# A streaming encoder layer: the high and low halves of the weights kept in memory after the first super-block

## The chip, the cores and the metric

The kernel runs on one core of a Trainium2 chip. The time is that of the device, in microseconds (us), from one execution of the whole program; the number given for a kernel is the median of several executions. The core has five engines that work side by side: PE (matrix products, with its weight loads shown apart as PEld), DVE (vector operations), ACT (activation functions and copies), POOL (general elementwise operations) and SP, which in this kernel does nothing but issue transfers between the large memory and the on-chip buffers. Each engine takes its instructions in the order in which they were written for it, and waits for semaphores that other engines or transfers raise.

## The reference, cut to what matters

One layer of a hybrid encoder on x of 2048 rows by 1024 channels, all in 32-bit floating point:

```python
shift, scale, gate = split(silu(c) @ w_ada + b_ada, 3)
h = rmsnorm(x, pre_g) * (1 + scale) + shift
q_lat, kv_lat, k_rope, gm_in, rw_in, z, g_logit = split(h @ w_in)     # 1024 -> 7712
y_mla = latent attention, 8 heads, chunk-causal                       # w_uq, w_ukv
y_gm  = gated spatial mixing inside blocks of 128 rows
y_rw  = RWKV-7 time mixing, 8 heads of 64, a scan over the rows       # w2, a2
branches = stack([y_mla, y_gm, y_rw]) * silu(z)
proj  = branches @ w_br                                               # 3 x (512 -> 1024)
merged = sum(proj * sigmoid(g_logit))
x = x + gate * rmsnorm(merged @ w_out, post_g)                        # 1024 -> 1024
```

The weights w_in, w_br, w_out, w_uq and w_ukv do not depend on the rows, so every block of rows multiplies by the same ones.

## The kernel before, in words

**Tiling.** The 2048 rows are handled in four super-blocks of 512 rows (`NSB`, `SB`). Activations stand transposed: channels on the 128 partitions, the 512 rows of a super-block along the free axis. A product with a large weight is done by `gemm` (lines 577 to 593): for a block of 128 output columns it takes 512 input channels at a time, one weight tile of 128 partitions x 4 x 128, and issues twelve matmuls on it.

**Twelve, because each factor is split in two.** PE multiplies in a format with fewer bits than 32-bit floats (fp32r). A value is therefore written as a high half, which is the value rounded to that format, and a low half, which is the rest; `mm3` (lines 572 to 575) adds high x high, high x low and low x high. The activations' halves are made once per super-block. The weights' halves are made by `wgran` (lines 562 to 570) every time a tile is used: a transfer of 256 KB from `w_in`, `w_br` or `w_out` into a raw tile `wr`, a copy on ACT into `wh`, and a subtraction on POOL or DVE into `wl` (`split`, lines 554 to 560). There are three buffers of each of `wr`, `wh` and `wl` (`WRB`, `WHB`). A super-block uses 162 such tiles: 120 of `w_in` and two for the rotary key (`rope_key`, lines 784 to 806), 24 of `w_br`, 16 of `w_out`; four super-blocks make 648. The small weights of the attention's projections, in `query`, `keys` and `values` (lines 808 to 854), are loaded, split by `parts` and used in the same way, 14 per super-block.

**Stages.** After a start-up part, each super-block s has a scan stage, `wkv(s)`, and then an attention stage, `attention(s)`; after the last one comes `finish`. In the scan stage a chain of small dependent steps runs for each of four pairs of heads: `prepare`, then `inverses` (on DVE, tiles X and tx, with a round trip through memory before and after it: md, mb, xd, xtb), then `advance` and `states` (matmuls into `pss`, with DVE and ACT between them: QG, UV, S, Y). Beside the chain PE does gemms of the projections, of the gates and of the branches' outputs. In the attention stage scores, softmax and weighted sums are on the chain, and gemms of the next super-block's inputs fill in.

**Order.** PE's instructions are in an order written out when the program is built: the class `Pace` (lines 93 to 323) keeps a model of all engines and of the transfers, has several threads of work with ranks, and each time takes the step that its model says can go first. The bookkeeping `pace.forget(h, l)` makes it never wait for weight halves. Which of POOL and DVE makes a low half is chosen from the backlogs in this model. The instructions of the other engines are ordered by a scheduler from dependencies and priorities; the loads in `wgran` are issued with a raised priority. SP issues nearly all transfers, in one queue.

In the profile nearly every instruction carries line 123, that of the wrapper that records it for `Pace`; so groups are told apart by the names of their tiles.

Of the kernel before, what the change touches and what calls it, by code (L numbers as in the profile page):

```python
# [22 lines left out]
P = 128  # L23
# [303 lines left out]
def trunk(ctx, tc, io, out):  # L327
# [231 lines left out]
            e = V if pace.backlog("Pool") + 1.25 > pace.backlog("DVE") + .6 + BIAS else G  # L559
        e.tensor_tensor(out=lo, in0=src, in1=hi.bitcast(F32), op=ALU.subtract)  # L560

    def wgran(src):

        raw = wp.tile([P, 4, P], F32, tag="wr", name="wr", bufs=WRB)
        with tc.high_priority(offset=100):
            SY.dma_start(raw, src.rearrange("(k p) c -> p k c", p=P))
        h = wp.tile([P, 4, P], F32R, tag="wh", name="wh", bufs=WHB)
        l = wp.tile([P, 4, P], F32R, tag="wl", name="wl", bufs=WHB)
        split(h, l, raw)
        return h, l  # L570

    def mm3(o, lh, ll, rh, rl, start, stop):
        PE.matmul(o, lh, rh, start=start, stop=False)
        PE.matmul(o, lh, rl, start=False, stop=False)
        PE.matmul(o, ll, rh, start=False, stop=stop)

    def gemm(w, c0, rhs, nk=KD, r0=0):

        yield (RD, *rhs[0])
        pace.lock = pace.cur  # L580
        o = pd()
        for kg in range(nk // 4):
            pace.early = EAR
            h, l = wgran(w[r0 + kg * 512:r0 + (kg + 1) * 512, c0:c0 + P])
            pace.early = 0.0
            pace.forget(h, l)
            for k in range(4):
                kk = kg * 4 + k
                rh, rl = rhs[kk]
                yield (rh, rl)  # L590
                mm3(o, h[:, k, :], l[:, k, :], rh, rl, kk == 0, kk == nk - 1)
        pace.lock = None
        return o
# [136 lines left out]
    def mla_units(s, pl):  # L730
        st = {}
        ts_ = slice(s * SB, (s + 1) * SB)

        def lng():
            return pl.tile([P, 512], F32, tag="lng", name="lng", bufs=4)

        def parts(x, hi, lo):
            A.activation(hi, x, AF.Copy)
            split_lo(lo, x, hi)
            return hi, lo  # L740

        def wparts():
            return [pl.tile([P, 2, P], F32R, tag=n, name=n, bufs=2) for n in ("wuqh", "wuql")]

        def weights(w):
            return parts(w, *wparts())

        def first():
            yield ()
            st["trig"] = trig_of(s, pl)  # L750

        def lat(i):
            o = yield from gemm(w_in, O_Q + i * P, hT)
            x = st[i] = lng()
            A.activation(x, o, AF.Copy)
            sq = st["s", i] = mt(pl, "sq")
            A.activation(sq, o, AF.Square)

        def norms():

            yield (RT, *(st["s", i] for i in range(3)))
            o = pt()
            for j in range(4):
                for c, ids in ((0, (0, 1)), (1, (2,))):
                    for i in ids:
                        PE.matmul(o[:, c * 4 + j:c * 4 + j + 1], st["s", i][:, j * P:(j + 1) * P], ones[:, 0:1],
                                  start=i == ids[0], stop=i == ids[-1])
            ms = sm.tile([P, 8], F32, tag="mss", name="mss")
            V.tensor_scalar(ms[:, 0:4], o[:, 0:4], 1.0 / 256, None, op0=ALU.mult)
            V.tensor_scalar(ms[:, 4:8], o[:, 4:8], 1.0 / 128, None, op0=ALU.mult)  # L770
            rs = sm.tile([P, 8], F32, tag="mrs", name="mrs")
            rstd_of(rs, ms, 1.0, EPS, 8)
            for c, ids, vec in ((0, (0, 1), "mla_q_norm"), (1, (2,), "mla_kv_norm")):
                dg = mt(pl, "dg")
                for j in range(4):
                    V.tensor_scalar(dg[:, j * P:(j + 1) * P], ident, rs[:, c * 4 + j:c * 4 + j + 1], None, op0=ALU.mult)
                yield (RT, dg)
                o = pt()
                PE.matmul(o, ones, dg, start=True, stop=True)
                for n, i in enumerate(ids):  # L780
                    V.scalar_tensor_tensor(st[i], st[i], col[vec][:, n:n + 1], o, op0=ALU.mult, op1=ALU.mult)
                    st[i] = parts(st[i], *(pl.tile([P, 512], F32R, tag=n, name=n, bufs=3) for n in ("lh", "ll")))

        def rope_key():
            yield (RD, *hT[0])
            pace.lock = pace.cur
            o = pd()
            for kg in range(2):
                pace.early = EAR
                raw = wp.tile([P, 4, P], F32, tag="wr", name="wr", bufs=WRB)  # L790
                SY.dma_start(raw[:, :, 0:96], w_in[kg * 512:(kg + 1) * 512, O_KR - 64:O_KR + 32].rearrange("(k p) c -> p k c", p=P))
                G.tensor_copy(raw[:, :, 96:112], raw[:, :, 80:96])
                G.tensor_copy(raw[:, :, 112:128], raw[:, :, 64:80])
                h = wp.tile([P, 4, P], F32R, tag="wh", name="wh", bufs=WHB)
                l = wp.tile([P, 4, P], F32R, tag="wl", name="wl", bufs=WHB)
                split(h, l, raw)
                pace.early = 0.0
                pace.forget(h, l)
                for k in range(4):
                    rh, rl = hT[kg * 4 + k]  # L800
                    yield (rh, rl)
                    mm3(o, h[:, k, :], l[:, k, :], rh, rl, kg + k == 0, kg * 4 + k == 7)
            pace.lock = None
            kp, t2 = mt(pl, "kp"), mt(pl, "t2")
            rope(kp[64:96], o, st["trig"], kp[64:96], t2[64:96])
            SY.dma_start(kp_d[s], kp[64:96])

        def query(h):
            wuq = pl.tile([P, 2, P], F32, tag="wuq", name="wuq", bufs=2)
            SY.dma_start(wuq[:, :, 0:96], io["mla_w_uq"][0, :, h * 96:(h + 1) * 96].rearrange("(i p) c -> p i c", p=P))  # L810
            G.tensor_copy(wuq[:, :, 96:112], wuq[:, :, 80:96])
            G.tensor_copy(wuq[:, :, 112:128], wuq[:, :, 64:80])
            wh, wl = weights(wuq)
            pace.forget(wuq, wh, wl)
            yield (RT, *st[0], *st[1])
            o = pt()
            for i in range(2):
                mm3(o, wh[:, i, :], wl[:, i, :], *st[i], i == 0, i == 1)
            q, t2 = mt(pl, "q"), mt(pl, "t2")
            A.activation(q[0:64], o[0:64], AF.Copy)  # L820
            rope(q[64:96], o, st["trig"], q[64:96], t2[64:96])
            SY.dma_start(q_d[s][h], q[0:96])

        def keys(hp):
            raw = pl.tile([P, 2, P], F32, tag="wuq", name="wk", bufs=2)
            w = raw[:, 0]
            src = io["mla_w_ukv"][0, :, hp * 256:(hp + 1) * 256].rearrange("p (h c) -> p h c", h=2)
            SY.dma_start(w.rearrange("p (h c) -> p h c", h=2), src[:, :, 0:64])
            wh, wl = wparts()
            parts(w, wh[:, 0], wl[:, 0])  # L830
            wl = wl[:, 0]
            pace.forget(raw, wh)
            yield (RT, *st[2])
            o = pt()
            mm3(o, wh[:, 0], wl, *st[2], True, True)
            k = mt(pl, "k")
            A.activation(k, o, AF.Copy)
            SY.dma_start(k_d[s][2 * hp:2 * hp + 2].rearrange("h d t -> (h d) t"), k)

        def values():  # L840
            src = io["mla_w_ukv"][0].rearrange("p (h c) -> p h c", h=8)
            w = []
            for i in range(2):
                raw = pl.tile([P, 2, P], F32, tag="wuq", name="wv", bufs=2)
                SY.dma_start(raw.rearrange("p a (h c) -> p (a h) c", h=2), src[:, i * 4:(i + 1) * 4, 64:128])
                w.append([x.rearrange("p a b -> p (a b)") for x in weights(raw)])
            for j in range(4):
                yield (RT, *w[0], *w[1], *st[2])
                o = pt()
                for i in range(2):  # L850
                    mm3(o[:, i * 256:(i + 1) * 256], *(x[:, j * P:(j + 1) * P] for x in st[2]), *w[i], True, True)
                v = mt(pl, "vv")
                A.activation(v, o, AF.Copy)
                SY.dma_start(v_d[s][j * P:(j + 1) * P, :], v)

        return ([first] + [lambda i=i: lat(i) for i in range(3)] + [norms, rope_key]
                + [lambda h=h: query(h) for h in range(8)] + [lambda h=h: keys(h) for h in range(4)] + [values])


# [879 lines left out]
```

## Time and profile before

| | |
|---|---|
| median of 3 runs | 3199.84 us (3196.55 to 3200.46) |
| profiled execution | 3196.95 us, span 3195.2 us |
| mean granted clock of PE | 0.959 |
| PE busy | 2952.7 us, 92% |
| PEld, DVE, ACT, POOL busy | 75%, 61%, 47%, 36% |
| transfers | 432.72 MB, mean 135 GB/s; 47.3% of 16 DMA engines on SP's queue |

The busy time of an engine is the time in which it executes an instruction. Matmuls are pipelined, so a busy PE is not PE at its peak. The granted clock is the share of PE's full clock of 2.4 GHz that the chip gave; it has two levels, 1.2 and 2.4 GHz, and a mean between 0.5 and 1 says how much of the time was spent at each. A wait is idle time of an engine before an instruction, put down to what ended it. The DMA share is the mean busy share of the core's 16 DMA engines.

### The profile page before, as it was taken

The page shows a single profiled execution, that of the slowest core. Times are in us where ns is not written, and L with a number is a line of the kernel's source. Part 1 is how long each engine was busy: PE and PEld are TensorE (multiplying, and loading weights), DVE is VectorE, ACT ScalarE, POOL GpSimd, SP SyncE. Part 2 cuts the span into 40 slices and gives each one's busy share as a digit, 9 for nine tenths or more (in the row PEclk, how much of TensorE's full clock was granted, in tenths as well). Part 3 has the DMA queues.
Part 4 walks back from the last instruction along what each step waited for, and adds up shares of the span by engine and source line. Part 5 has one row for each costly group of instructions (what it writes and reads, how often), then busy time and mean ns, then how long its engine had stood idle before and what let it go on. Part 6 is the DMA issues. An engine that isn't in the chain of part 4 may idle for free.

```text
span 3195.2 us, 47968 instructions
## 1 busy us (share of the span) xinstructions
PE 2952.7 (92%) x16156; PEld 2403.9 (75%) x16156; DVE 1933.3 (61%) x4703; ACT 1490.1 (47%) x3334; POOL 1157.7 (36%) x1083
## 2 busy tenths in 40 slices
PE   5899989899989989989999998999899999899998
PEld 4677767788777778877877776887687777688886
DVE  6435764574576755467376765557636676466663
ACT  4334332554434436554443435555444344277753
POOL 2343333452433333333443334334234332233333
PEclk8999899999999999989999999999999999899999
DMA  7444333754543566443553456444345436543345
GB/s 247 134 121 111 80 90 87 198 146 131 167 123 105 146 179 180 137 131 109 161 163 100 129 164 183 113 128 134 99 115 154 124 110 171 153 112 90 99 129 163
DMA packets 594114, 432.72 MB, mean 135 GB/s; under 512 B 143216, under 2 KB 489420, under 8 KB 593868
## 3 DMA queue, kind: packets, MB, share of 16 engines
q1 hardware_dynamic: 593696, 429.62, 47.3%
q8 instruction: 127, 2.08, 0.3%
q14 instruction: 119, 0.97, 0.1%
q10 hardware_dynamic: 172, 0.05, 0.0%
HBM read 328.61 MB, written 100.93 MB: 134 GB/s over the span
## 4 chain that ended last, share of the span: by engine, by line
PE 56%; DVE 12%; DMA 4%; issue 3%; ACT 2%; POOL 1%; SPq 0%; DVEq 0%; POOLq 0%; ACTq 0%
PE pd L123 34%; PE pss L123 10%; PE pst L123 9%; PE pso L123 4%; DVE X L123 2%; DMA x<-in_x 2%; DVE tx L123 1%; DVE y L123 1%; DVE q L123 1%; SPq L123 0%; DMA stg<-q_d 0%; DVE wl L123 0%; DVE gt L123 0%; ACT p L123 0%; DVE t L123 0%
## 5 line engine op out<-in xcount | busy, mean ns | idle before, releaser
L123 POOL TENSOR_TENSOR wl<-wr,wh 128x512 fp32r<-128x512 f32 x479 | 633.0, 1323 | 1217.3 <-ACT wh L123 1166.1
L123 PE MATMUL pd<-hh,wh 128*128 128x512 f32 x1952 | 816.6, 418 | 8.5 <-ACT hh L123 2.8
L123 PE MATMUL pd<-hl,wh 128*128 128x512 f32 x1952 | 775.3, 397 | 2.5 <-DVE hl L123 1.5
L123 PE MATMUL pd<-hh,wl 128*128 128x512 f32 x1952 | 774.3, 397 | 0.0
L123 ACT ACTIVATE wh<-wr 128x512 fp32r<-128x512 f32 x648 | 406.5, 628 | 777.7 <-PE pd L123 493.7
L123 PEld LDWEIGHTS pd<-hh,wh 128*128 128x128 f32 x1952 | 374.8, 192 | 93.7 <-ACT wh L123 7.7
L123 PEld LDWEIGHTS pd<-hh,wl 128*128 128x128 f32 x1952 | 373.1, 191 | 83.4
L123 PEld LDWEIGHTS pd<-hl,wh 128*128 128x128 f32 x1952 | 375.0, 192 | 69.1 <-DVE hl L123 3.5
L123 DVE TENSOR_TENSOR pw<-pst,ph 128x512 fp32r<-128x512 f32 (+2 forms) x352 | 195.8, 566 | 178.7 <-ACT ph L123 176.8
L123 PE MATMUL pd<-brh,wh 128*128 128x512 f32 x576 | 255.1, 443 | 18.0 <-DVE lastp L123 12.4
L123 ACT ACTIVATE ph<-pst 128x512 fp32r<-128x512 f32 (+2 forms) x352 | 171.4, 495 | 185.4 <-PE pst L123 142.9
L123 PE MATMUL pd<-brh,wl 128*128 128x512 f32 x576 | 235.1, 408 | 1.9 <-DVE wl L123 1.9
L123 PE MATMUL pd<-brl,wh 128*128 128x512 f32 x576 | 235.5, 409 | 0.5 <-DVE brl L123 0.5
L123 DVE TENSOR_SCALAR_CACHE_REDUCE p<-pss 128x512 f32<-128x512 f32 (+2 forms) x320 | 192.0, 606 | 59.8 <-PE pss L123 56.1
L123 ACT ACTIVATE p<-p,nm 128x512 f32<-128x512 f32 (+3 forms) x288 | 189.6, 660 | 57.3 <-DVE nm L123 57.2
L123 DVE TENSOR_TENSOR wl<-wr,wh 128x512 fp32r<-128x512 f32 x169 | 139.3, 825 | 81.1 <-ACT wh L123 79.4
L123 PE MATMUL pst<-consts,p 128*128 128x128 f32 x1088 | 164.8, 276 | 17.9 <-DVE ri L123 7.1
L123 PEld LDWEIGHTS pst<-consts,p 128*128 128x128 f32 x1088 | 130.1, 142 | 37.8 <-DVE ri L123 7.8
L123 PE MATMUL pso<-ph,v 128*128 128x256 f32 x576 | 153.1, 287 | 0.0
L123 PEld LDWEIGHTS pd<-brh,wh 128*128 128x128 f32 x576 | 114.3, 198 | 49.8 <-issue 12.7
L123 PE MATMUL pso<-pw,v 128*128 128x256 f32 x576 | 147.3, 284 | 3.7 <-DVE pw L123 3.7
L123 PE MATMUL pss<-kh,qh 96*128 96x512 f32 (+2 forms) x320 | 130.2, 407 | 13.7 <-ACT kh L123 13.7
(296 smaller groups left out, 5205.3 us busy)
## 6 DMA issues: line engine op xcount, KB each, us to landing
wr<-in_w_in SPq DMA_DIRECT2D x480, 256.0 KB
wr<-in_w_br SPq DMA_DIRECT2D x96, 256.0 KB
gate_d<-gt SPq DMA_DIRECT2D x64, 256.0 KB
part_d<-gt SPq DMA_DIRECT2D x64, 256.0 KB
p<-part_d SPq DMA_DIRECT2D x64, 256.0 KB
wr<-in_w_out SPq DMA_DIRECT2D x64, 256.0 KB
x<-in_x SPq DMA_DIRECT2D x56, 256.0 KB
gt<-gate_d SPq DMA_DIRECT2D x56, 256.0 KB
```

What stands on the lines that cost most here:

```text
L123: r = f(*a, **k)
```

## The change

In the first super-block every weight tile is split as before, and both halves are then stored in memory, each in a tensor of its own (`keep`). In the other three super-blocks the two halves are loaded instead of the raw tile, and nothing is split (`again`). The loaded halves go into the buffers of all three kinds in turn: the high and the low half of successive tiles take a `wr` and a `wh` buffer, a `wl` and a `wr` buffer, a `wh` and a `wl` buffer, so that the nine buffers hold four and a half pairs. The weights of the rotary key and the small weights of the attention's projections are treated alike; `keys` takes two pairs of heads with one small weight now, which makes 12 instead of 14 per super-block.

```diff
-    def wgran(src):
+    kept = {}
+
+    def keep(key, h, l):
+        kept[key] = [dr.tile(list(x.shape), F32, name="kept") for x in (h, l)]
+        for d, x in zip(kept[key], (h, l)):
+            SY.dma_start(d, x.bitcast(F32))
+
+    def again(key, h, l):
+        with tc.high_priority(offset=100):
+            for d, x in zip(kept[key], (h, l)):
+                SY.dma_start(x.bitcast(F32), d)
+
+    turns = [0]
+
+    def wgran(key, fill):
+        if key in kept:
+            tags = [("wr", "wh"), ("wl", "wr"), ("wh", "wl")][turns[0] % 3]
+            turns[0] += 1
+            h, l = (wp.tile([P, 4, P], F32R, tag=g, name="wh" if n == 0 else "wl", bufs=WHB) for n, g in enumerate(tags))
+            again(key, h, l)
+            return h, l
         raw = wp.tile([P, 4, P], F32, tag="wr", name="wr", bufs=WRB)
         with tc.high_priority(offset=100):
-            SY.dma_start(raw, src.rearrange("(k p) c -> p k c", p=P))
+            fill(raw)
         h = wp.tile([P, 4, P], F32R, tag="wh", name="wh", bufs=WHB)
         l = wp.tile([P, 4, P], F32R, tag="wl", name="wl", bufs=WHB)
         split(h, l, raw)
+        keep(key, h, l)
         return h, l
...
-            h, l = wgran(w[r0 + kg * 512:r0 + (kg + 1) * 512, c0:c0 + P])
+            src = w[r0 + kg * 512:r0 + (kg + 1) * 512, c0:c0 + P].rearrange("(k p) c -> p k c", p=P)
+            h, l = wgran((w.tensor.name, w.offset, r0 + kg * 512, c0), lambda raw: SY.dma_start(raw, src))
...
-        def weights(w):
-            return parts(w, *wparts())
+        def weights(key, fill):
+            hl = wparts()
+            if key in kept:
+                again(key, *hl)
+                return hl
+            w = pl.tile([P, 2, P], F32, tag="wuq", name="wuq", bufs=2)
+            fill(w)
+            parts(w, *hl)
+            keep(key, *hl)
+            return hl
...
         def keys(hp):
...
+            if hp % 2 == 0:
+                src = io["mla_w_ukv"][0, :, hp * 256:(hp + 2) * 256].rearrange("p (a h c) -> p (a h) c", a=2, h=2)
+                wk[:] = weights(("k", hp), lambda raw: SY.dma_start(raw.rearrange("p a (h c) -> p (a h) c", h=2), src[:, :, 0:64]))
+                pace.forget(*wk)
             yield (RT, *st[2])
             o = pt()
-            mm3(o, wh[:, 0], wl, *st[2], True, True)
+            mm3(o, wk[0][:, hp % 2], wk[1][:, hp % 2], *st[2], True, True)
```

`rope_key`, `query` and `values` pass what fills their raw tile in the same way.

## Rows read from the trace of the kernel before

**Rows 1.** Stretches in us: length, busy PE, PEld, DVE, ACT, POOL (instructions), clock, DMA share, GB/s

```profile
0.00:206.00 206.00, 154.62 (x651) 119.50 (x652) 101.88 (x155) 74.02 (x135) 67.48 (x78) 0.92 0.58 177
206.00:575.00 369.00, 344.09 (x1983) 271.94 (x1982) 227.40 (x569) 141.23 (x276) 132.60 (x109) 0.96 0.36 94
575.00:812.00 237.00, 220.62 (x1122) 184.30 (x1121) 136.72 (x344) 120.52 (x285) 103.59 (x114) 0.95 0.56 158
812.00:1187.00 375.00, 349.66 (x2034) 277.10 (x2033) 252.94 (x609) 149.54 (x341) 135.08 (x111) 0.97 0.51 145
1187.00:1562.00 375.00, 355.75 (x1824) 295.80 (x1823) 208.49 (x532) 196.26 (x445) 142.10 (x149) 0.96 0.50 139
1562.00:1943.00 381.00, 356.38 (x2044) 283.04 (x2043) 255.18 (x610) 150.39 (x343) 135.19 (x111) 0.96 0.51 143
1943.00:2384.00 441.00, 411.88 (x2191) 346.44 (x2190) 251.49 (x622) 249.04 (x563) 165.93 (x170) 0.97 0.45 126
2384.00:2784.00 400.00, 369.27 (x2095) 290.23 (x2093) 253.44 (x620) 153.71 (x350) 133.30 (x111) 0.96 0.50 144
2784.00:3110.00 326.00, 318.61 (x1900) 277.92 (x1901) 212.31 (x599) 227.91 (x545) 110.34 (x100) 0.98 0.39 109
3110.00:3196.00 86.00, 71.77 (x328) 57.61 (x327) 33.45 (x46) 27.52 (x54) 32.03 (x33) 0.95 0.51 165
```

**Rows 2.** Costliest groups: out<-in, shapes, xcount | busy us, mean ns | idle before

```profile
L123 POOL TENSOR_TENSOR wl<-wr,wh 128x512 fp32r<-128x512 f32 x479 | 633.0, 1323 | 1217.3 <-ACT wh L123 1166.1
...
L123 ACT ACTIVATE wh<-wr 128x512 fp32r<-128x512 f32 x648 | 406.5, 628 | 777.7 <-PE pd L123 493.7
...
L123 DVE TENSOR_TENSOR wl<-wr,wh 128x512 fp32r<-128x512 f32 x169 | 139.3, 825 | 81.1 <-ACT wh L123 79.4
```

**Rows 3.** PE's waits from 935 us on: us in total, times, longest

```profile
PE pss L123 <- DVE QG L123: 17.7, 7, 4.5
PE pss L123 <- ACT kh L123: 10.5, 3, 5.2
...
PE pd L123 <- DVE wl L123: 1.9, 2, 1.7
```

**Rows 4.** Tiles X and QG: xcount: duration ns min/median/max, first and last start

```profile
L123 DVE TENSOR_TENSOR X<-X,tx x368: 154/223/1910, 256.7 to 2685.2; 128x60 f32<-128x60 f32 x24, 128x66 f32<-128x66 f32 x16, 128x69 f32<-128x69 f32 x8, 128x63 f32<-128x63 f32 x8
...
L123 DVE TENSOR_TENSOR QG<-pss,ard x64: 405/422/429, 322.5 to 2745.3; 64x256 f32<-64x256 f32 x64
```

**Rows 5.** Timeline near 1053 us: start us, us, engine, operation

```profile
1053.26 1.80 POOL L123 TENSOR_TENSOR wl<-wr,wh 128x512 fp32r<-128x512 f32 x1 [0.71 <-ACT wh L123]
...
1053.82 1.28 DVE L123 TENSOR_TENSOR X<-X,tx 128x28 f32<-128x28 f32 x1
```

**Rows 6.** Timeline of ACT in a dense stretch, with the idle time before

```profile
1536.71 0.63 ACT L123 ACTIVATE wh<-wr 128x512 fp32r<-128x512 f32 x1 [2.09 <-PE pd L123]
...
1542.15 0.63 ACT L123 ACTIVATE wh<-wr 128x512 fp32r<-128x512 f32 x1 [2.09 <-PE pd L123]
```

**Rows 7.** The page's DMA queues: packets, MB, share of 16 engines

```profile
q1 hardware_dynamic: 593696, 429.62, 47.3%
```

**Rows 8.** The stretch 20 to 28 us, as in rows 1

```profile
20.00:28.00 8.00, 3.19 (x11) 2.08 (x12) 8.00 (x8) 5.96 (x10) 1.75 (x1) 1.00 1.03 412
```

**Rows 9.** Chain of waits: start us, us, what

```profile
655.94 2.18 DMA wr<-in_w_in
...
2147.44 3.63 DMA wr<-in_w_br
```

**Rows 10.** Tile wr: SP's issues (duration ns), and idle time that ended with a load

```profile
L123 SPq DMA_DIRECT2D wr<-in_w_in x488: 367/379/3045, 24.5 to 3000.4; - x163
...
  DMA wr<-in_w_in: 19.5, 12
```

**Rows 11.** SP's waits: us in total, times, longest

```profile
SPq L123 <- POOL wl L123: 969.4, 376, 16.2
...
SPq L123 <- POOL gt L123: 87.7, 31, 10.7
```

More of the change, by code (lines that the diff above doesn't have):

```diff
@@ L789, in rope_key, with fill @@
                 pace.early = EAR
[L790 to L796, printed above, removed]
+                def fill(raw):
+                    SY.dma_start(raw[:, :, 0:96], w_in[kg * 512:(kg + 1) * 512, O_KR - 64:O_KR + 32].rearrange("(k p) c -> p k c", p=P))
+                    G.tensor_copy(raw[:, :, 96:112], raw[:, :, 80:96])
+                    G.tensor_copy(raw[:, :, 112:128], raw[:, :, 64:80])
+                h, l = wgran(("kr", kg), fill)
                 pace.early = 0.0
@@ L808, in query, with fill @@
         def query(h):
[L809 to L814, printed above, removed]
+            def fill(wuq):
+                SY.dma_start(wuq[:, :, 0:96], io["mla_w_uq"][0, :, h * 96:(h + 1) * 96].rearrange("(i p) c -> p i c", p=P))
+                G.tensor_copy(wuq[:, :, 96:112], wuq[:, :, 80:96])
+                G.tensor_copy(wuq[:, :, 112:128], wuq[:, :, 64:80])
+            wh, wl = weights(("q", h), fill)
+            pace.forget(wh, wl)
             yield (RT, *st[0], *st[1])
@@ L822, in query @@
             SY.dma_start(q_d[s][h], q[0:96])
+        wk = []
         def keys(hp):
[L825 to L832, printed above, removed]
+            if hp % 2 == 0:
+                src = io["mla_w_ukv"][0, :, hp * 256:(hp + 2) * 256].rearrange("p (a h c) -> p (a h) c", a=2, h=2)
+                wk[:] = weights(("k", hp), lambda raw: SY.dma_start(raw.rearrange("p a (h c) -> p (a h) c", h=2), src[:, :, 0:64]))
+                pace.forget(*wk)
             yield (RT, *st[2])
             o = pt()
-            mm3(o, wh[:, 0], wl, *st[2], True, True)
+            mm3(o, wk[0][:, hp % 2], wk[1][:, hp % 2], *st[2], True, True)
             k = mt(pl, "k")
@@ L843, in values @@
             for i in range(2):
-                raw = pl.tile([P, 2, P], F32, tag="wuq", name="wv", bufs=2)
-                SY.dma_start(raw.rearrange("p a (h c) -> p (a h) c", h=2), src[:, i * 4:(i + 1) * 4, 64:128])
-                w.append([x.rearrange("p a b -> p (a b)") for x in weights(raw)])
+                hl = weights(("v", i), lambda raw: SY.dma_start(raw.rearrange("p a (h c) -> p (a h) c", h=2), src[:, i * 4:(i + 1) * 4, 64:128]))
+                w.append([x.rearrange("p a b -> p (a b)") for x in hl])
             for j in range(4):
```

## The prediction

> **What bounds the kernel now.** I read the table of stretches first, then the groups, the waits, and last the timeline of one dense stretch. The table shows one engine near its limit, PE, busy 2952.7 us of 3196 when its ten rows are added, and where it idles [rows 1]. The stretches alternate between a scan stage (206 to 575, 812 to 1187, 1562 to 1943, 2384 to 2784) and an attention stage, one pair per super-block, and a tail. From 812 us to the end PE idles 25.3 + 19.3 + 24.6 + 29.1 + 30.7 + 7.4 + 14.2 = 150.7 us. In the same stretches the granted clock is 0.95 to 0.98, a mixture of the levels 1.2 and 2.4 GHz; (1 - clock) times the length of each, summed, is 81.5 us of PE time lost to the low level.
>
> The groups show what the change takes away [rows 2]: 648 copies on ACT that form the high half, and 648 subtractions, 479 on POOL and 169 on DVE, that form the low half. None bounds anything by its busy time. PE's own waits [rows 3] after 935 us are short and mostly on DVE: 16 rows that name a DVE result, from 17.7 us (QG) down to 1.9 us, add up to about 95 us. Four rows name ACT, the largest 10.5 us (kh), about 18 us together. A wait for a weight half appears with 1.9 us in two cases. So weights are ready in time today; what makes PE idle is DVE, late in the scan's chain.
>
> **Why the splits matter though they are off the chain.** X, a step of the scan's chain on DVE, takes 223 ns at the median and 1910 ns at worst; QG, which reads PSUM, never leaves 405 to 429 ns [rows 4]. One X step that took 1.28 us lies inside a POOL subtraction of 1.80 us [rows 5]. So POOL's subtractions delay DVE steps of this kind, and DVE is in order: what PE waits for (QG, Y, lastp) stands behind them. In the dense stretch each ACT copy is preceded by 2.09 us of waiting for PE to free a buffer [rows 6], with ACT's later work queued behind the copy.
>
> **The change, part by part.**
>
> *Splits gone in super-blocks 1 to 3.* Three of four tiles, 486 of 648, are no longer split: 0.75 x 406.5 = 305 us off ACT, 0.75 x 633.0 = 475 us off POOL, 0.75 x 139.3 = 104 us off DVE [rows 2]. PE's work stays. What can be won is its idle time of 150.7 us and the clock. Bounds: nothing, if the order of PE's instructions, fixed when the kernel is built by a model of the engines, leaves the same holes; 150.7 us if all holes close. In 812 to 3196 DVE is busy 1467 us [rows 1]; 104 us is 7% of that, and the blocked steps come on top. I take half of the 95 us on DVE and of the 18 us of waits on ACT in the same answer, so -57 us. Half, because QG, the largest, is not itself slowed, only what stands ahead of it. After this the late part is PSUM eviction by DVE and ACT, which the change leaves. The 12 small weights per super-block of the attention's projections go the same way and are in this term.
>
> *Clock.* If the low level shrinks with the idle time, 57 / 150.7 x 81.5 = -31 us. Bounds 0 and -81.
>
> *Two stores per tile in the first super-block.* 324 stores of 256 KB on SP's queue, each behind its split. 138 of the 162 tiles have their first use before 812 us; 24 (the merge and the output projection) in the next scan stage. The price of a 256 KB transfer on all 16 DMA engines: over the whole kernel 47.3% of 3195.2 us for 429.62 MB is 0.92 us per 0.262 MB; in the stretch 20 to 28, DMA full at 412 GB/s, 0.64 us [rows 7, 8]. So 276 stores take 177 to 254 us of an 812 us stretch in which DMA is now busy about 385 us (0.58, 0.36 and 0.56 of its parts [rows 1]): 0.69 to 0.79. Not full, and the cover is PE's matmuls. What pays is a transfer on the scan's chain that finds a store pair in front of it, 1.3 to 1.8 us each. Four heads with four round-trip transfers each would pay 20 to 29 us, if all were hit. ACT's copy into a high-half buffer must also wait for the store of three tiles earlier; the store needs about as long as a load, 2.18 to 3.63 us [rows 9], and PE holds the buffer 2.72 us for its own tile and longer ahead of it, so that mostly hides. I take +15 us; bounds 0 and +60.
>
> *Loads.* Instead of one load with 512-byte pieces, two contiguous ones. 486 more transfers are 311 to 447 us on DMA; from 812 us on its share goes from 0.48 to 0.61 to 0.67. SP issues 810 more DMAs of 0.379 us [rows 10], 307 us, on a queue that today spends 969.4 us waiting for POOL's subtraction to free the raw buffer [rows 11]. That wait becomes one for PE: a load is issued when the tile 4 or 5 places earlier is done. Behind it on SP stand the spills, the attention's loads and the scan's round trips, as they stand behind POOL's subtraction now.
>
> *Are the halves in time?* In the dense stretch two ACT copies 5.44 us apart bracket two tiles, so 2.72 us per tile [rows 6]; three tiles cover 8.16 us. Needed: two issues, 0.76 us, one landing, 2.18 to 3.63 us [rows 9], the second transfer, 0.64 to 0.92 us: 3.6 to 5.3 us. At least 2.9 us to spare. SP can be held longer: on POOL's gt it waits 87.7 us in 31 cases, 10.7 us at worst [rows 11]. Before, the raw load and the split had separate buffers and six tiles of lead; only 19.5 us in 12 cases were waited for a raw load [rows 10]. I take +15 us, with 0 and +120 as bounds.
>
> Two weight loads on the chain of waits landed in 2.18 us and in 3.63 us [rows 9]. The Trainium skill (HBM Reference, Latency) gives an access 0.2 us on average and 2 us under high load; no run here shows an access alone. Its 1.8 us more would make the need 5.4 to 7.1 us, an estimate from that page, so that a hold of SP of 1.1 us would already stop PE, and the late-halves rival below would be likelier.
>
> *The order of PE.* The model that places PE's instructions sees fewer bookings on ACT, POOL and DVE and more on DMA, so the order changes everywhere after the first tiles. That can go either way by some 15 us; I count 0.
>
> **Sum.** -57 - 31 + 15 + 15 = -58 us against the profiled execution's own 3196.95 us (span 3195.2 and 1.75 around it): 3139 us. The median of the runs shown, 3199.84, is 2.9 us above that execution: 3142 us.
>
> **Rivals.**
> A. *The holes stay* (nothing to win). PE is 92% busy and its order is fixed; in the last attention stage it idles only 7.4 of 326 us [rows 1]. For: the waits are 1 to 4 us each, the size of errors of the model. Against: X's slow tail comes from POOL. Then only the costs and some DVE time remain: 3190 to 3210 us, 3200.
> B. *Everything DVE and ACT delay goes.* -113 us of waits, clock in proportion -61, costs +30: 3197 - 144 + 3 = 3056 us. For: DVE and ACT lose a large part of their in-order queues. Against: QG's own time.
> C. *The halves come late* (slower than before). Place: gemm tiles of super-blocks 1 to 3, when SP stands behind a spill whose producer is late, and the two loads leave too late for the 8.16 us of cover. Price: 2 us per late tile on PE, times 1.54 for the clock (81.5 / 150.7 more): 40 late tiles, one reload in 12, are +123 us; with -88 and +15 as above, 3197 + 50 + 3 = 3250 us. It decides from about 24 late tiles (24 x 3.1 = 74 us, more than the 73 us otherwise won). For: SP's long holds [rows 11]. Against: today's loads are late in 12 cases of 648.
>
> **Chances.** Forecast (3090 to 3185) 0.52, A 0.12, B 0.14, C 0.22. About 0.2% (6 us) is what a measurement of this kernel can tell from no change. A falls into it with 0.08, and with 0.02 on each side: faster 0.68, same 0.08, slower 0.24. The range leaves out half of B and about half of C: 3065 to 3240 us.
>
> **What the changed profile would show.** Right: POOL's subtraction group down to about 120, ACT's copies to 162; X's maximum rarely above 0.5 us after 1200 us; PE idle in the three later scan stages near 50 us instead of 80.6; granted clock up by 0.01. DMA at 0.7 to 0.8 before 812 us. Wrong: PE or its weight loads waiting on a DMA of the kept halves for more than 30 us in all (C), the same waits on DVE after 935 us as now (A), or PE idle before 812 us up by over 40 us (the stores).

## The result and the profile after

The changed kernel takes 3148.65 us (median of four, 3144.93 to 3157.4), the kernel before 3198.53 us beside it (3196.55 to 3200.46): a ratio of 0.9848, with the 95% interval 0.9825 to 0.9871. The prediction was 3142 us. The profiled execution took 3146.36 us, with a span of 3144.4 us and a mean granted clock of 0.964 (before 0.959).

The stretches of the kernel after, cut at the same starts of stages as in [rows 1], with the same columns:

```profile
0.00:234.00 234.00, 179.14 (x738) 137.57 (x738) 108.64 (x168) 80.93 (x144) 57.90 (x70) 0.92 0.85 273
234.00:618.00 384.00, 349.67 (x2027) 277.38 (x2026) 231.80 (x591) 146.29 (x282) 109.93 (x92) 0.97 0.72 224
618.00:840.00 222.00, 197.97 (x987) 165.99 (x988) 121.06 (x322) 95.06 (x226) 56.06 (x58) 0.90 0.65 202
840.00:1213.00 373.00, 354.59 (x2077) 281.63 (x2076) 222.16 (x603) 117.12 (x282) 67.52 (x62) 0.97 0.71 226
1213.00:1563.00 350.00, 333.38 (x1742) 278.74 (x1741) 177.20 (x492) 148.14 (x350) 67.84 (x72) 0.98 0.65 203
1563.00:1921.00 358.00, 346.17 (x2054) 276.74 (x2054) 211.84 (x595) 102.70 (x257) 42.30 (x42) 0.98 0.68 213
1921.00:2355.00 434.00, 413.85 (x2202) 348.89 (x2201) 220.65 (x589) 199.56 (x467) 86.28 (x89) 0.97 0.59 184
2355.00:2705.00 350.00, 341.53 (x2047) 272.93 (x2046) 211.79 (x595) 102.61 (x257) 42.59 (x42) 0.99 0.69 217
2705.00:3020.00 315.00, 309.76 (x1862) 271.17 (x1861) 191.14 (x573) 207.31 (x505) 74.70 (x72) 0.99 0.46 137
3020.00:3145.00 125.00, 100.95 (x435) 80.51 (x433) 35.34 (x55) 17.02 (x36) 16.34 (x20) 0.91 0.68 227
```

Subtract PE's busy time from each length, and take (1 - clock) times the length for the time lost to the low level, as the prediction did:

| | before | after | change |
|---|---|---|---|
| PE idle before the second scan stage (812 / 840 us) | 92.7 | 113.2 | +20.5 |
| lost to the low clock there | 43.1 | 52.4 | +9 |
| PE idle from there on | 150.7 | 104.7 | -46 |
| lost to the low clock there | 81.5 | 56.3 | -25 |

The four add up to -41.5 us of the span's -50.8; the other 9 us I can't place (the clock has two digits, and that alone is worth some 10 us over 2300 us). So the three later super-blocks gain about 71 us and the first gives about 30 back.

What left the queues, in the columns of [rows 2]:

```profile
L123 POOL TENSOR_TENSOR wl<-wr,wh 128x512 fp32r<-128x512 f32 x96 | 129.2, 1347 | 442.1 <-ACT wh L123 362.9 <-PE pd L123 30.6 <-DMA kept<-wh 9.5
...
L123 ACT ACTIVATE wh<-wr 128x512 fp32r<-128x512 f32 x162 | 101.5, 628 | 220.0 <-PE pd L123 75.7 <-DMA kept<-wh 60.6 <-DMA wr<-in_w_in 16.0
...
L123 DVE TENSOR_TENSOR wl<-wr,wh 128x512 fp32r<-128x512 f32 x66 | 48.6, 737 | 100.3 <-ACT wh L123 63.1 <-DMA kept<-wl 32.0 <-PE pst L123 5.0
```

PE's waits from 840 us on, the longest in sum first (compare [rows 3], where QG had 17.7 us):

```profile
PE pss L123 <- ACT kh L123: 11.5, 3, 5.0
PE pd L123 <- DVE gt L123: 10.0, 7, 4.4
...
PE pss L123 <- DVE QG L123: 3.4, 3, 2.8
```

And SP's waits, as in [rows 11], with the wait of ACT's copies for the stores below:

```profile
SPq L123 <- PE pd L123: 734.7, 358, 14.1
...
SPq L123 <- POOL wl L123: 76.1, 64, 3.1
...
ACT wh L123 <- DMA kept<-wh: 60.6, 31, 4.5
```

The reader is to see three things. The splits are a quarter of what they were. SP, which stood 969.4 us behind POOL's subtraction, now stands 734.7 us behind PE: the wait has moved, as forecast. And no row of PE's waits from 840 us on names a kept half; its weight loads waited for one once, for 0.4 us.

The queue of transfers carries half as much again as in [rows 7]:

```profile
q1 hardware_dynamic: 524544, 651.06, 65.9%
```

### The profile page after: what moved, and what is told of

It is laid out like the page before. It is cut to its first block, busy times and chain, and to the rows that moved or that the text cites. A ratio compares the mean times of both kernels' runs of the same rounds, so it can differ in the third digit from the quotient of the medians.

```text
span 3144.4 us, 47954 instructions
## 1 busy us (share of the span) xinstructions
PE 2927.0 (93%) x16156; PEld 2391.6 (76%) x16156; DVE 1731.6 (55%) x4578; ACT 1216.7 (39%) x2806; POOL 621.5 (20%) x618
## 5 line engine op out<-in xcount | busy, mean ns | idle before, releaser
L123 PE MATMUL pd<-hh,wh 128*128 128x512 f32 x1952 | 814.5, 417 | 19.3 <-ACT wh L123 10.3
L123 POOL TENSOR_TENSOR wl<-wr,wh 128x512 fp32r<-128x512 f32 x96 | 129.2, 1347 | 442.1 <-ACT wh L123 362.9
L123 ACT ACTIVATE wh<-wr 128x512 fp32r<-128x512 f32 x162 | 101.5, 628 | 220.0 <-PE pd L123 75.7
L123 POOL TENSOR_TENSOR kl<-stg,kh 96x512 fp32r<-96x512 f32 x80 | 103.8, 1300 | 223.8 <-ACT kh L123 194.6
```

Source lines behind the costliest of these rows:

```text
L123: r = f(*a, **k)
```

## The experiments

Each ratio is to the kernel before, run beside it, with its 95% interval. **Theory Q**: the time comes from the in-order queues of DVE, POOL and ACT, freed of splits, above all because POOL's subtractions no longer delay DVE. **Rival O**: it comes from PE's new order, because the planner replans everything. **Rival D**: it comes from the loads (contiguous, and no longer behind the split). The stores' cost is asked apart.

### Stand-ins for the splits put back into the kernel after

Three runs add instructions that read the reloaded halves and write where nobody reads. The planner is not told, so PE's order stays that of after.

```diff
             again(key, h, l)
+            nc.scalar.activation(dum[0], h.bitcast(F32), AF.Copy)                              # e1, e3
+            e, d = (nc.vector, dum[2]) if turns[0] % 4 == 0 else (nc.gpsimd, dum[1])           # e1, e2
+            e.tensor_tensor(out=d, in0=h.bitcast(F32), in1=l.bitcast(F32), op=ALU.subtract)    # e1, e2
             return h, l
```

> The changed kernel, with one ACT copy and one subtraction (POOL three times in four, DVE once) of each reloaded pair into tiles that nobody reads, 486 of each; they do no part of the computation, and the model that orders PE is not told of them, so PE's order stays that of the changed kernel. Theory Q (the gain is the engines' queues freed from splits): the late stretch gives back its 46 us of idle time and 25 us of low clock, so 3148 becomes about 3215, at least 3190. Theory O (the gain is a better order of PE, planned with fewer bookings) and theory D (the gain is that halves come in longer pieces): it stays at 3145 to 3160.

> As the run before, with the 486 subtractions alone. Theory Q with POOL delaying DVE as the cause (X takes up to 1.9 us beside a subtraction): most of the loss of both, 3185 to 3205. If ACT's copies are the cause: 3145 to 3165.

> As the run before the last, with the 486 copies on ACT alone. Theory Q with POOL and DVE as the cause: 3150 to 3170. With ACT as the cause: 3185 to 3205.

Measured: both 3291.12 us (1.0286, 1.0262 to 1.0309); the subtractions alone 3260.92 us (1.021, 1.0191 to 1.0229); the copies alone 3176.43 us (0.9934, 0.9918 to 0.9949). Against after's 0.9848 the subtractions cost 0.0362 x 3198 = 116 us, the copies 27 us, both 140 us. The direction is Q's, the sizes are not what I expected: with the subtractions more comes back than the change had taken away, and they weigh four times what the copies do. These runs alone do not rule D out: all three have after's loads, but a stand-in may cost time that a split did not. What speaks against D are the waits. From the start of the second scan stage on PE waited for no load in before, and 1.9 us for a weight half. From there on DVE's waits on loads did not fall with the change (49.5 us in before, 65.0 us in after), nor did ACT's (84.9 and 105.5 us). No run changes the loads alone.

A fourth run, on another occasion, puts all subtractions on DVE:

```diff
-            e, d = (nc.vector, dum[2]) if turns[0] % 4 == 0 else (nc.gpsimd, dum[1])
+            e, d = nc.vector, dum[2]
```

> Kernel after, with one extra subtraction per reloaded pair that reads both halves, all 486 on DVE and none on POOL (in e2_low_back 365 ran on POOL and 121 on DVE). D1, what counts is the time taken from DVE's in-order queue, by its own instructions or by those of POOL that block it: e2 took 94 us of own and about 130 us of blocked time and cost 112 us; this takes 486 x 0.69 = 335 us and no blocked time, so 112 x 335 / 224 = 168 us: about 3315 us (3280 to 3340). D2, what counts is that POOL makes DVE steps of the scan's chain slow, or holds POOL's own queue: both are gone, and 335 us are spread over a DVE that is 55% busy: 3150 to 3210 us. In between: both.

Measured: 3215.24 us (1.0048, 1.0027 to 1.0069), 64 us above after. D1's 3315 us is out, D2's 3150 to 3210 us just missed. Now the pages. In the first line of each, DVE was busy 1731.6 us in after, 1907.2 us with the mixture of e2, 2031.5 us with e5. So 176 us more of busy DVE cost 116 us, and 300 us more cost 64 us. Of the 176 us only 94 are e2's own stand-ins; the other 82 us (the expectation above had about 130) are other DVE steps that took longer. DVE time as such is not the dear part; DVE time lost beside POOL is. One thing the stand-ins have that the splits had not: each stands in its engine's queue until its reloaded halves have landed. In e5 DVE sat idle for that 264.7 us in 193 cases, in e2, from 850 us on, 113.1 us in 47, and part of that idle time would have been there anyway. So the 116 and 64 us may be more than the splits themselves cost; that e2 is the slower of the two is not explained by it, since e5 waits longer. The sums of PE's waits (all rows of the waits view, from the start of the second scan stage) say who makes PE wait:

| kernel | on DVE, us (times) | on ACT | on POOL |
|---|---|---|---|
| before | 110.5 (88) | 20.9 (16) | 6.6 (6) |
| after | 59.7 (51) | 23.8 (16) | 3.3 (3) |
| e3, copies | 72.6 (63) | 27.0 (20) | 3.3 (3) |
| e5, subtractions on DVE | 101.8 (85) | 24.1 (17) | 2.7 (3) |
| e2, subtractions, three in four on POOL | 123.7 (86) | 27.3 (22) | 3.0 (3) |

Two rows of e2, which stand for that sum (PE's waits from 855 us on):

```profile
PE pd L123 <- DVE gt L123: 19.2, 10, 4.4
PE pso L123 <- DVE ak L123: 18.1, 7, 4.9
```

Though 365 of e2's subtractions run on POOL, PE hardly waits for POOL (3.0 us). Nor does DVE wait much longer for POOL's results: 38.2 us in after, 45.7 us in e2, 40.7 us in e5 (from the start of the second scan stage). POOL's own queue is thus at most a small part. What grows are DVE's steps beside POOL's subtractions. The DVE steps on tile X, 696 in each kernel, from 850 us on (length, busy us, clock, DMA share, GB/s; after, e2, e5):

```profile
850.00:3300.00 2450.00, 167.98 (x696) 0.98 0.59 186
850.00:3300.00 2450.00, 201.80 (x696) 0.97 0.60 187
850.00:3300.00 2450.00, 165.74 (x696) 0.97 0.60 187
```

In before the same line has 204.19 us, in e9 below 173.75 us. Counted in the timelines from 1200 us on, 39 of the 368 steps X and tx took over 0.5 us in before, 8 in after, 29 in e2, 7 in e5 and 14 in e9. In before 27 of the 39 began inside a weight subtraction of POOL; all 8 of after began inside POOL steps of the scan. That a blocked step weighs more than a queued one because it sits on the scan's chain is my reading; no run blocked steps of another kind.

### The stores alone, in the kernel before

The 160 tiles of `gemm` are stored in the first super-block and never read again; the planner is not told.

```diff
+    def keep(key, h, l):
+        kept[key] = [dr.tile(list(x.shape), F32, name="kept") for x in (h, l)]
+        for d, x in zip(kept[key], (h, l)):
+            nc.sync.dma_start(d, x.bitcast(F32))
...
         split(h, l, raw)
+        if key not in kept:
+            keep(key, h, l)
```

> The kernel before, with the 320 stores of the halves at each tile's first use (w_in, w_br, w_out; the rotary key's two tiles left out) and nothing loaded back; the model is not told of them, so PE's order is that of before. The first super-block of the changed kernel lost about 20 us of idle time and 9 us of clock. If the stores themselves do that (transfers, buffers held until a store lands): 3198 becomes 3215 to 3230. If the loss is the new order's: 3195 to 3205.

Measured: 3215.44 us (1.0057, 1.004 to 1.0073), 18 us more; the prediction took +15. Its stretches (columns as in [rows 1]) against 815 us to the end of the first attention stage and 378 us for the second scan stage in the kernel before:

```profile
0.00:826.00 826.00, 725.74 (x3771) 580.16 (x3772) 460.15 (x1070) 338.03 (x697) 302.04 (x301) 0.94 0.70 219
826.00:1224.00 398.00, 362.69 (x2043) 286.08 (x2041) 256.59 (x610) 151.34 (x343) 135.74 (x112) 0.94 0.58 170
```

11 us are lost before 826 us, with DMA at 0.70, and 20 us in the next scan stage, where only the last 24 tiles are stored; the rest is 7 us shorter (1995 against 2002 us). The trace is that of the slowest of six executions (3221.24 us), so its parts add up to 24 us and not 18.

### Planned or not planned

Two kernels hide something from the planner. The work executed is the same, in another order; which of POOL and DVE makes a low half, which is chosen from the planner's backlogs, shifts with it (e6: 127 on POOL and 35 on DVE, after 96 and 66; e8: 495 and 153, before 479 and 169).

```diff
-            SY.dma_start(d, x.bitcast(F32))          # e6, in keep() of the kernel after
+            nc.sync.dma_start(d, x.bitcast(F32))
...
-        split(h, l, raw)                             # e8, in wgran() of the kernel before
+        nc.scalar.activation(h, raw, AF.Copy)
+        e = nc.vector if pace.backlog("Pool") + 1.25 > pace.backlog("DVE") + .6 + BIAS else nc.gpsimd
+        e.tensor_tensor(out=l, in0=raw, in1=h.bitcast(F32), op=ALU.subtract)
```

> Kernel after, with the stores hidden from the model that plans the order of PE; they are still issued. If the 20 us that PE idles more before 840 us come from an order planned around the stores, this kernel is faster: 3125 to 3140 us. If they come from the stores themselves (buffers held, the transfers in front of others), it is the same or slower: 3145 to 3175 us.

> Kernel before, with its splits hidden from the model that plans the order of PE: all 648 tiles are still split by ACT and by POOL or DVE, nothing is stored. It tells whether after gains by the order that was planned without splits (O) or by the queues that no longer run them (Q). O: 3150 to 3170 us. Q: not faster than before, 3200 to 3300 us.

Measured: e6 3132.32 us (0.9806, 0.9778 to 0.9834), so 13 to 16 us below after, though the intervals still touch. It is the fastest version seen. Its trace cannot show where the time went, for its profiled execution, at 3147.65 us, is one of two among six that were no faster than after. e8 3202.88 us (1.0016, 1.0000 to 1.0032). An order planned without splits gives nothing while the splits are there: O is refuted as the source. The next two runs ask the same of after's own order.

### The two orders exchanged

The planner's choices were recorded in one kernel and replayed in the other, so that each kernel does its own work with PE in the order of the other (apart from a few steps with the attention's small weights, which the change regroups).

```diff
     def run(self, until, share=0.0, spare=lambda: True):
-        ... (the model picks the thread that can go first)
+        for n in PICKS.pop(0):
+            best = [th for th in self.threads if th[3] == n][0]
+            r = self.ready(best)
+            self.t = max(self.t, r if r < self.INF else 0.0)
+            self.step(best)
```

> Kernel after, with PE's work in the order of the kernel before (the list of the planner's choices in before is replayed, 5096 steps). It splits what after gains into freed queues and re-planning. Q, the freed queues pay in any order: e4_stores_only put stores alone at 3215 us in this order, after is 67 us below that, and nearly all of it stays: 3150 to 3175 us. P, the freed time pays only where PE's order is planned for it: the holes stay as they are, 3195 to 3215 us.

> Kernel before, with PE's work in the order of the kernel after (the planner's choices in after are replayed; every tile is split, nothing is stored). e1_splits_back had this order with stand-in splits and took 3291 us. If the stand-ins cost what splits cost, 3265 to 3300 us. If e1 was slow because a reloaded pair was split besides, and the order itself is as good as that of before for split weights, 3195 to 3230 us.

Measured: e9 3155.26 us (0.9865, 0.9843 to 0.9886); e10 3246.72 us (1.0158, 1.0135 to 1.0181). This is the table that settles what the order has to do with it:

| | order of before | order of after |
|---|---|---|
| tiles split four times | 1 | 1.0158 |
| the same, with the stores | 1.0057 | not run |
| the change | 0.9865 | 0.9848 |

In the order of before the change wins 43 us, and 61 us (0.0192 x 3199) if it is set against the kernel that pays for the stores too. Replanning adds 5 us, less than the intervals tell apart. In the unchanged order PE's waits on DVE from the second scan stage on fall from 110.5 us in 88 cases to 71.4 us in 64, those on ACT rise from 20.9 to 30.9 us. With the order of after the change wins 0.031 x 3198 = 99 us, the stores' price included: an order made without splits stands them badly, which is one reason why e1 and e2 brought back more than the change had won. The other is that e1's stand-ins seem to cost more than splits do: e10 is some 40 us faster than e1, of which the stores, which only e1 has, may be 18. It lies between my two ranges (3195 to 3230 and 3265 to 3300 us). Like the change itself, e9 and e10 differ from their partners in splits, loads and stores together; that the gain is the splits' and not the loads' rests on the waits and on e1 to e3.

Where each order gains, from four traces, cut at the start of the second scan stage (before; e9; e10; after):

```profile
0.00:815.00 815.00, 722.33 (x3769) 578.34 (x3770) 467.74 (x1070) 336.81 (x697) 303.68 (x301) 0.95 0.47 134
815.00:3195.00 2380.00, 2230.33 (x12389) 1825.55 (x12387) 1465.57 (x3634) 1153.32 (x2638) 853.97 (x782) 0.96 0.48 136
```

```profile
0.00:821.00 821.00, 722.97 (x3762) 573.97 (x3763) 456.27 (x1070) 315.32 (x647) 238.63 (x232) 0.96 0.75 238
821.00:3152.00 2331.00, 2207.93 (x12396) 1809.70 (x12394) 1270.86 (x3498) 900.73 (x2157) 395.00 (x397) 0.97 0.63 197
```

```profile
0.00:845.00 845.00, 734.50 (x3794) 591.71 (x3795) 455.73 (x1065) 344.32 (x704) 310.99 (x308) 0.94 0.46 131
845.00:3248.00 2403.00, 2228.13 (x12364) 1824.00 (x12362) 1463.39 (x3633) 1147.02 (x2632) 853.44 (x781) 0.96 0.47 134
```

```profile
0.00:844.00 844.00, 730.78 (x3779) 584.62 (x3780) 464.32 (x1083) 322.28 (x652) 224.80 (x220) 0.94 0.74 232
844.00:3144.00 2300.00, 2196.23 (x12379) 1806.95 (x12377) 1267.29 (x3496) 894.44 (x2154) 396.66 (x399) 0.97 0.64 199
```

PE's instructions in the first part agree within 32. In the order of after that part takes 844 us with the stores and 845 us without them; in the order of before 821 and 815 us. So most of what after gives back early, 844 - 821 = 23 of the 29 us, is its order, and not the stores as such. The same order then wins 31 us in the rest (2300 against 2331), if no split is left. These are differences of one trace each, and executions of after alone lie up to 12 us apart. They fit e6, in which the planner is not told of the stores: there the part takes 830 us. That this is why e6 is faster is not shown, since its traced execution lost those 14 us again later.

### Buffers

```diff
-            tags = [("wr", "wh"), ("wl", "wr"), ("wh", "wl")][turns[0] % 3]
+            tags = ("wh", "wl")                                                       # e11, order of after replayed
...
-        h = wp.tile([P, 4, P], F32R, tag="wh", name="wh", bufs=WHB)
+        h = wp.tile([P, 4, P], F32R, tag="wh", name="wh", bufs=4)                     # e7, planned anew; e12, order of e6 replayed
```

> Kernel after, in its own PE order, with reloaded halves in the buffers of high and low halves only: three pairs in place of four and a half. The prediction's working: two tiles of 2.72 us cover 5.4 us where 3.6 to 5.3 us are needed, so little is lost in dense stretches: 3146 to 3170 us. If after is already near the point where halves come late (rival C), one and a half pairs less make a tile in six late by 2 us or more, 80 x 3.1 = 250 us: over 3250 us, and at least over 3190 us.

> Kernel after, with four buffers for the high halves in place of three. In after, ACT waits 60.6 us in 31 cases before a high-half copy until the store of the tile three places earlier has read its buffer. If that reaches PE in the first super-block, the fourth buffer takes 10 to 20 us off: 3128 to 3140 us. If it is hidden, as the prediction said, 3143 to 3155 us.

> Kernel e6_stores_unplanned in its own PE order (replayed), with a fourth buffer for the high halves. e7_four_high_buffers lost 35 us against after, with a fourth buffer and a PE order planned anew. If the new order lost them, the buffer alone does no harm here: 3120 to 3137 us. If the buffer itself loses them (copies that run further ahead and put POOL's and DVE's subtractions in front of other work): 3150 to 3175 us.

Measured: e11 3182.55 us (0.9947, 0.9928 to 0.9966), 32 us above after; e7 3183.23 us (0.9954, 0.9938 to 0.997), 34 us above after; e12 3144.32 us (0.9831, 0.9809 to 0.9853), between its two expectations and not told apart from e6.

e11 lies between what its two theories gave, and PE still hardly waits for a half (its weight loads 4.9 us in 9 cases). PE's waits and one of DVE's from 850 us on, and one of SP's over the whole execution:

```profile
PE pd L123 <- DVE gt L123: 12.7, 6, 5.8
...
PE pd L123 <- ACT gt L123: 8.0, 2, 4.6
...
PE pss L123 <- DMA xtb<-xd: 5.7, 3, 4.0
...
PE pd L123 <- DMA wl<-kept: 1.6, 4, 0.6
...
DVE gt L123 <- DMA gt<-gate_d: 35.9, 10, 9.9
...
SPq L123 <- PE pd L123: 794.8, 375, 14.2
```

In after the same rows have 10.0, 1.6, 2.0, none, 23.7 (7 cases) and 734.7 us. With fewer buffers SP stands 60 us longer before a reload whose buffer PE still reads, and the other loads of that queue, gates and the scan's round trips, come later. These rows make up only a part of e11's 32 us, so that SP's longer stand is the cause is likely, not shown. e7 shows that a plan made anew can cost two thirds of what the change brings: its first part takes 868 us, against 844 in after and 838 in e12, which has the same four buffers in another order. ACT's wait for the stores was barely shorter (52.7 us), so that wait was not tested by it.

## Why the prediction was right

**What bounds the kernel, and by what.** Right. PE's waits on DVE fell from 110.5 to 59.7 us, and e2 and e5 showed that the subtractions on POOL act through DVE. QG fell from 17.7 to 3.4 us, more than the half I took; in the unchanged order of e9 it fell to 9.2 us, which is that half. Two readings of rows were loose. The X step of [rows 5] starts inside POOL's subtraction and ends 0.04 us after it (1055.10 and 1055.06 us), and in [rows 6] only every second copy of ACT waits 2.09 us for PE; the copy between those two follows 1.60 us of waiting for POOL's subtraction. Neither is a term of the sum.

**Splits gone, with the clock (-57 and -31).** The direction is shown, the size was too large: 88 us were taken, and the change won 61 us in an unchanged order (e9 against e4). In after's trace the two terms come out as -46 and -25. The waits on ACT did not fall at all (20.9 to 23.8 us), though I had counted half of 18 us.

**Stores (+15).** 18 us by e4. DMA before 840 us is at 0.85, 0.72 and 0.65, as promised (0.7 to 0.8 together). "Mostly hides" was said of ACT's wait for the store three tiles earlier; it came to 60.6 us in 31 cases on ACT, while PE waited for ACT's copies 10.3 us in 5 cases.

**Late halves (+15), and rival C.** Not there: no wait of PE on a kept half from 840 us on, 0.4 us of its weight loads, and 1.6 and 4.9 us even with three pairs. What the lead seems to buy is SP's freedom, which I had named for the spills and not priced. C's place was wrong, its first link (SP stands behind PE) was right.

**Order of PE (0).** -5 us by e9 against after, within the intervals. It hides two parts of opposite sign, +23 us before 840 and -31 us behind it in the traces, and e7 (34 us) and e10 (50 us) show that a plan can be worth 30 to 50 us. The bound of 15 us was too narrow.

So -58 was forecast and -50 came: a gain put too high by some 25 us and a loss of 15 us that did not come partly cancel. That the sum came within 8 us is in part luck.

**The promised signs.** POOL's subtractions at 129.2 us (120 promised), ACT's copies at 162, PE idle in the three later scan stages 18.4 + 11.8 + 8.5 = 38.7 us (50 promised), the clock up by 0.005 (0.01 promised). X held: 6 of its 184 steps after 1200 us take over 0.5 us, 23 did in before. The longest still takes 1.79 us there, since other POOL work does the same. The tile and the timeline near 1646 us in after (columns as in [rows 4] and [rows 5]):

```profile
L123 DVE TENSOR_TENSOR X<-X,tx x368: 149/222/1901, 304.1 to 2634.9; 128x60 f32<-128x60 f32 x24, 128x66 f32<-128x66 f32 x16, 128x69 f32<-128x69 f32 x8, 128x63 f32<-128x63 f32 x8
```

```profile
1644.55 1.80 POOL L123 TENSOR_TENSOR r<-r,k 128x512 f32<-128x512 f32 x1 [7.41 <-DVE k L123]
...
1645.11 1.31 DVE L123 TENSOR_TENSOR X<-X,tx 128x60 f32<-128x60 f32 x1
...
1646.30 1.92 POOL L123 TENSOR_TENSOR bkb<-bk,E 128x1024 f32<-128x1024 f32 x1
...
1646.45 1.85 DVE L123 TENSOR_TENSOR tx<-X,mb 128x66 f32<-128x66 f32 x1
```

The X step, started inside r, ends 0.07 us after r (1646.42 and 1646.35 us), and the tx step 0.08 us after bkb (1648.30 and 1648.22). These are POOL's own steps of the scan, which the change leaves. The Trainium skill (SBUF — State Buffer, SBUF: two separate sides) has a rule for it: a DVE operation with two inputs in that memory and a GpSimd operation that reads it exclude each other for the whole of the one that started first. These rows agree, as does QG, which reads PSUM and kept to 405 to 429 ns [rows 4].

## What to carry to other kernels

Work taken from engines that are half idle can pay when it stood in the way of short steps on the chain; ask which engine's steps it delayed, and count the long ones among such steps; busy shares do not show it, and the longest duration stayed at 1.9 us here. Where an order is planned by a model, an edit's price has two parts, the work and the plan: replay the old order under the new work before saying which one was paid. And buffers for a prefetch may buy more than punctual data: with fewer of them (e11) the queue that issues the loads stood still 60 us longer, for all other transfers too.

## What the hardware showed that I had not expected

An addition of 176 us to DVE's busy time cost 116 us when POOL ran most of the added subtractions, and one of 300 us cost 64 us when DVE ran them all. With DMA at 0.63 from 850 us on, twice the bytes per tile did not make the halves late: even in e11 PE waited for them 1.6 us in sum, and its weight loads 4.9 us. And 320 stores beside the loads cost 18 us, though they raised DMA's share before 826 us from 0.47 to 0.70.
